# A diffusion trunk on one core: block differences and weight sums on VectorE, row sums in four column groups

## The chip, the core and the metric

The kernel runs on one core of a Trainium2 chip. A core has TensorE (PE in the profile), which multiplies matrices; VectorE (DVE) and ScalarE (ACT) for elementwise work; GpSimd (POOL), also elementwise here; and SyncE (SP), which issues most of the transfers. Each engine takes the instructions of its own queue in order; semaphores make one engine wait for another. TensorE reads its operands from the on-chip memory SBUF and writes to accumulators in PSUM, which VectorE or ScalarE have to read out before their place is used again. The metric is the device time of one execution in microseconds; less is better.

## The reference

One layer (DEPTH = 1) of a generator of latents: 2048 latent tokens and 256 context tokens of width 1024. An HGRN2 mixer with two scan directions over eight heads is followed by a gated FFN with a convolution; each part is preceded by an RMS norm with a shift and a scale that come from a conditioning vector.

```python
m_l = (sc_lat @ w_ada[l] + b_ada[l])[:, None, :]
sh1, sc1, g1, sh2, sc2, g2 = jnp.split(m_l, 6, axis=-1)
hl = modulate(rmsnorm(lat, norm_g[l, 0]), sh1, sc1)
...
# in the mixer:
q, zf_fwd, zf_bwd, v, g = jnp.split(h @ w_in, 5, axis=-1)
...
lat = lat + g1 * yl
hl = modulate(rmsnorm(lat, norm_g[l, 1]), sh2, sc2)
lat = lat + g2 * conv_ffn(hl, ffn_w_up[l], ffn_conv_w[l], ffn_conv_b[l], ffn_w_down[l])
```

The change touches two things: the projections to `v` and `g` (columns 3 and 4 of the five parts of `w_in`), which the early stage computes ahead of the mixer, and the rows `g1`, `sh2`, `sc2` and `g2` of the modulation, which are needed later.

## The kernel before

**Exact products from three passes.** Each operand is split into a high part that TensorE multiplies exactly enough and the rest: `split` (L80, L81) lets ScalarE copy the source to the high part and VectorE subtract that from the source. A product is then three matmuls: high by high, high by low, low by high.

**The early stage** (`early`, about the first 420 us) first computes the shift and scale of the first norm (L352, four column groups of 32 partitions into one accumulator), then normalizes, transposes and modulates the tokens, and multiplies them by the `v` and `g` weights of the heads. The multiplication is a Strassen-Winograd scheme of two by two blocks: tokens in two units by weights of a pair of heads, the inner width of 1024 in two halves. Seven block products per pair of heads take the place of eight; for them one needs differences of token blocks and sums of weight blocks:

- `differences(j)` (L450 to L455): for each of four slices j, two differences on VectorE (L450, L451), whose results are split at once into the factors T2 and T1, and two more on POOL (L454, L455), written over the tokens in `hm0`, which are split later into T3 and T4.
- `Blocks.sums` (L217, L218) makes S1 and S2 of the weight blocks, `sum3` (L223) makes S3 in the place of one raw block and `sum4` (L228) S4 in the place of S2. All four work on 128 x 512 floats, and all run on POOL.
- `product(g, p, n)` runs one block product of twelve matmuls (L515, L517, L518) for the pair p and then reads the accumulator out, with ScalarE (L526, L530, L544) or with an addition on VectorE (L546, L549, L551, L557). The accumulators have four tags (za, zc, zd, tr) with two buffers each. `turned_out` transposes a finished block on TensorE (L476) some steps later, copies it with ScalarE (L477) and stores it.

**Two halves.** The list `todo` holds the products. The first half (g = 1) takes tokens 1024 to 2047 with seven pairs of heads: four of `v` (`vs`) and three of `g` (`gs`). The second (g = 0) takes tokens 0 to 1023 with eight pairs, after `turn_over`. Raw weights come in by DMA into a few reused tiles (`load_raws`, L577); `prepare` asks for sums and splits four products ahead (`LOOK`). During the first half `side_tokens` also normalizes and transposes tokens 0 to 1023 (L130, L132, L139, L143), takes their differences on VectorE (L682 to L687) and stores them to memory, from where `load_factor` brings them back for the second half. The scale of a norm is a power on POOL (L76) between two VectorE instructions (L75, L132).

**The order** of each engine's queue isn't the order of the program text alone: a scheduler orders instructions by need and by its own estimate of when their inputs are there; `issue_after`, `behind_of` and `then` add edges that place one behind another, and `at(clock, f)` places work at a count of products.

**The later modulation rows** (`ada_rest`) run beside the second half: for each of four rows, VectorE accumulates eight slices of `w_ada` times the conditioning vector into `acc` (L725, L727); the row is the sum of `acc` over its 128 partitions. TensorE makes it by multiplying with a column of ones, in two products of 512 columns (L735), each into an accumulator of tag tr; ScalarE copies each to SBUF (L736), and SP stores the row to memory (L737).

Of the kernel before, what the change touches and what calls it, by code (L numbers as in the profile page):

```python
# [11 lines left out]
F32 = mybir.dt.float32  # L12
# [3 lines left out]
AF = mybir.ActivationFunctionType  # L16
OP = mybir.AluOpType
# [28 lines left out]
def body(ctx, tc, a, out):  # L46
    nc = tc.nc
    pe, act, dve, pool, sp = nc.tensor, nc.scalar, nc.vector, nc.gpsimd, nc.sync
# [4 lines left out]
    m_rows = [dr.tile([1, D], F32, name=f"m_row{i}") for i in range(4)]  # L53
# [13 lines left out]
    def small(name, shape=(128, 8), dt=F32):  # L67
        return cst.tile(list(shape), dt, name=name)
# [10 lines left out]
    def split(h, l, src):  # L79
        i = act.activation(h, src, AF.Copy)  # L80
        j = dve.tensor_tensor(l, src, h.bitcast(F32), OP.subtract)  # L81
        return i.ins, j.ins
# [13 lines left out]
    def pool_(stack, name, bufs=1, **kw):  # L96
        return stack.enter_context(tc.tile_pool(name=name, bufs=bufs, reuse_waits="tile", **kw))
# [66 lines left out]
    G_PLAIN = NH - 2  # L164
# [39 lines left out]
    class Blocks:  # L204


        def __init__(self, ring):
            self.ring, self.w = ring, {}

        def raws(self, raw):  # L210
            self.raw = raw
# [19 lines left out]
        def split(self, n, w=None):  # L231
            if n in self.w:
                return
            if n == "S3" and n not in self.src:
                self.sum3()
            if n == "S4" and n not in self.src:
                self.sum4("S2")
            if w is None:
                w = self.ring()
            self.w[n] = w  # L240
            return split(w[:, 0], w[:, 1], self.src[n])
# [3 lines left out]
            return act.activation(hm, tp, AF.Identity, bias=B1[m][:, k:k + 1], scale=A1[m][:, k:k + 1])  # L245
        return dve.tensor_scalar(hm, tp, A1[m][:, k:k + 1], B1[m][:, k:k + 1], OP.mult, OP.add)

    ones = small("ones", (128, 1))
    pool.memset(ones, 1.0)

    def early():
# [4 lines left out]
        pb = pool_(ce, "pb", 2)  # L256
# [15 lines left out]
        def factor_tile(n):  # L272
            f = left_place if n in LEFT_PLACE else place
            return f({**PLACE, **LEFT_PLACE}[n], TOK, F32R, "r" + n)

        def half_tile(tag, bufs, name=None):
            return pb.tile([128, UT, 128], F32, name=name or tag, tag=tag, bufs=bufs)
# [71 lines left out]
        for k in range(KT):  # L349
            for c in range(4):  # L350
                n = 2 * k + c // 2
                pe.matmul(mp[32 * c:32 * c + 32], silp[:, k],  # L352
                          ada[n // 4][:, n % 4, c % 2 * 512:(c % 2 + 1) * 512],
                          start=k == 0, stop=k == KT - 1, skip_group_check=True)
# [24 lines left out]
        def split_ctx(g):  # L379
            b = cxt[:, g // 2, :, :, 2 * (g % 2):2 * (g % 2) + 2]  # L380
            return split(b[:, :, 0], b[:, :, 1], hmc[g].rearrange("p k s n -> p s k n"))
# [8 lines left out]
        ps = pool_(ce, "pse", 2, space=PSUM)  # L390
# [22 lines left out]
        def z_tile(tag):  # L413
            return ps.tile([128, UT, 128], F32, name=tag, tag=tag)

        hm0 = px.tile([128, KT, UT, 128], F32, name="hm0", tag="X", bufs=1)
        rhs = {}

        def unit0(k):

            tp = z_tile("tr")
            turn_tok(tp.rearrange("p (i j) n -> p i j n", i=1), range(HT, HT + UT), (k,))
            hm = hm0[:, k]
            i = modulated(hm, tp, k, 0, k % 2 == 0).ins
            b = block(0, k // 4)[:, :, :, k % 4]
            return split(b[:, :, 0], b[:, :, 1], hm)
# [17 lines left out]
        def differences(j):  # L444

            if j == 0:
                for n in ("T2", "T1", "T3", "T4"):
                    rhs[n] = factor_tile(n)
            a12, a22 = hm1[j], hm1[j + 4]
            dve.tensor_tensor(a12, a12, hm0[:, j], OP.subtract)  # L450
            dve.tensor_tensor(a22, a22, a12, OP.subtract)  # L451
            put_split("T2", j, a22)
            put_split("T1", j, a12)
            pool.tensor_tensor(hm0[:, j], a22, hm0[:, j], OP.subtract)  # L454
            pool.tensor_tensor(hm0[:, j + 4], hm0[:, j + 4], a22, OP.subtract)  # L455

        def put_split(n, j, src):
            split(rhs[n][:, :, 0, j], rhs[n][:, :, 1, j], src)
# [32 lines left out]
        for p in range(4):  # L491
# [10 lines left out]
            z = z_tile("zc").rearrange("p (i s) n -> p i s n", i=2)  # L502
            for i in range(2):
                context_row(p, i, z[:, i])
            o = half_tile("out", 4)
# [72 lines left out]

        class Heads(Blocks):

            def __init__(self, ty, h):
                super().__init__(ring)
                self.ty, self.h, self.z, self.summed = ty, h, {}, False

            def first_half(self, tile):
# [4 lines left out]
            def prepare(self, n):  # L590
                if LEFT[n] in self.w:
                    return
                if n[0] == "T" and not self.summed:
                    self.summed = True
                    self.sums(pool, *[pb.tile([128, 4, 128], F32, name=n, tag=n) for n in ("s1", "s2")])
                self.split(LEFT[n])

        todo = []
        vs = [Heads(3, 2 * i) for i in range(4)]
        for p, b in zip(vs, vb):  # L600
            p.w.update({n: b.w[n] for n in ("A11", "A12")})
        gs = [Heads(4, h) for h in range(0, G_PLAIN, 2)]
        for p in gs[0:2]:
            p.first_half(rawp.tile([128, D], F32, name="raw", tag="raw"))
        at(c0 + 21, lambda: gs[2].first_half(lp.tile([128, D], F32, name="raw", tag="stg", bufs=1)))
# [13 lines left out]
        todo += [(1, p, n) for n in FACTORS[2:] for p in gs[0:2]]  # L619
        turn_over = len(todo)  # L620
        for i, (ty, h) in enumerate(((3, 0), (3, 4), (4, 0), (4, 4))):
            both = [Heads(ty, h), Heads(ty, h + 2)]
            loads[len(todo) - 12] = both, i % 2 == 0
            todo += [(0, p, n) for n in FACTORS for p in both]

# [4 lines left out]
        def unit1_step(i):  # L630
            k = (0, 4, 1, 5, 2, 6, 3, 7)[i]
            then(unit1, k)
            if i % 2:
                differences(k - 4)
# [16 lines left out]
        def side_tokens(j, now):  # L651
# [41 lines left out]
            for i, (u, g) in enumerate(((0, 0), (0, 1), (1, 0), (1, 1))):  # L693
                at(now + 8 + 2 * i, lambda u=u, g=g: turn(u, g))
            at(now + 17, differences)
            at(now + 19, differences2)

# [5 lines left out]
        def spare_raw():  # L703
            if not spare:
                spare.extend([hq.tile([128, 4, D], F32, name="spare", tag="cxt", bufs=1), 0])
            spare[1] += 1
            return spare[0][:, (spare[1] - 1) % 4]

        def ada_rest():

            def load(n):
                i, k = divmod(n, KT)
                raw = spare_raw()
                sp.dma_start(raw, a["w_ada"][k * 128:(k + 1) * 128, (2 + i) * D:(3 + i) * D])
                return raw

            ahead = [load(n) for n in range(2)]
            yield
            for i in range(4):
                acc_ = lp.tile([128, D], F32, name="acc", tag="stg", bufs=1)  # L720
                for k in range(KT):
                    raw = ahead.pop(0)
                    s_ = sil[:, k:k + 1]
                    if k:
                        dve.scalar_tensor_tensor(acc_, raw, s_, acc_, OP.mult, OP.add)  # L725
                    else:
                        dve.tensor_scalar(acc_, raw, s_, None, OP.mult)  # L727
                    if k == KT - 1:
                        row = spare_raw()[0:1]
                    if KT * i + k + 2 < 4 * KT:  # L730
                        ahead.append(load(KT * i + k + 2))
                    yield
                for n in range(2):
                    z = ps.tile([1, 512], F32, name="z", tag="tr")
                    pe.matmul(z, ones, acc_[:, n * 512:(n + 1) * 512], start=True, stop=True)  # L735
                    act.activation(row[:, n * 512:(n + 1) * 512], z, AF.Copy)  # L736
                sp.dma_start(m_rows[i], row)  # L737
                yield

        rest = ada_rest()  # L740
        factor_raw = []

# [134 lines left out]
    first_out = []  # L877

    early()
    clock, at, run, tick = ticking()  # L880
    Sf = hp.tile([128, NH, 128], F32, name="Sf", tag="Sf", bufs=1)
# [559 lines left out]
    def cols(u, odd):  # L1441

        return u[:, 1:1 + HALF].rearrange("p (j o n) -> p j o n", o=2, n=128)[:, :, odd]
# [307 lines left out]
    ps = pool_(fp, "psa", 2, space=PSUM)  # L1751
# [94 lines left out]
    ring = {}  # L1846
# [53 lines left out]
    for g, (half, s, n, q, pairs) in enumerate(todo):  # L1900
# [9 lines left out]
        if n == "B11":  # L1910
            z = bank["a", q] = ps.tile([128, HJ, 128], F32, name="za", tag="za")
# [3 lines left out]
        elif n == "T2":  # L1915
            z = ps.tile([128, HJ, 128], F32, name="zb", tag="zb")
            acc_mm(z, w, r, True)
            dve.tensor_tensor(u2s[q], u2s[q], z, OP.add)
        elif n == "T1":
            z = bank["d", q] = ps.tile([128, HJ, 128], F32, name="zd", tag="zd")  # L1920
            acc_mm(z, w, r, True)
            uvs[q] = u_tile(wk, "v")
            i = dve.tensor_tensor(cols(uvs[q], 1), u2s[q], z, OP.add).ins
# [4 lines left out]
        elif n == "T3":  # L1928
            z = bank["c", q] = ps.tile([128, HJ, 128], F32, name="zc", tag="zc")
            acc_mm(z, w, r, True)  # L1930
            dve.tensor_tensor(cols(uvs[q], 1), cols(uvs[q], 1), z, OP.add)
        elif n == "B21":
            z = bank["a", q]
# [3 lines left out]
        elif n == "B22":  # L1937
            z = bank["d", q]
            acc_mm(z, w, r, False)
            dve.tensor_tensor(cols(ugs[q], 1), u2s[q], z, OP.add)  # L1940
        else:
            z = bank["c", q]
# [15 lines left out]
    ps = pool_(fb, "psb", 8, space=PSUM)  # L1958
# [176 lines left out]
    for s in range(N):  # L2135
        ph, c = divmod(s, NC)
# [62 lines left out]
    for i, (j, cs) in enumerate(pieces):  # L2199
        prepare_last(i + 2)  # L2200
        if cs.start == 0:
            z = ps.tile([128, 512], F32, name="y", tag="y")
# [36 lines left out]
```

## Time and profile before

| | |
|---|---|
| median of three runs | 2717.66 us |
| lowest and highest | 2716.46 and 2718.87 us |
| the profiled execution | 2719.17 us |
| its span from the first to the last instruction | 2717.5 us |
| TensorE busy in the span | 98% |
| granted TensorE clock, mean | 0.994 |
| TensorE busy, 0 to 34 us (first shift and scale) | 18.07 of 34 us |

In a row of instruction groups one reads line, engine, operation, result and inputs, shapes, the count, then busy time and the mean duration in nanoseconds, and last the idle time of that engine just before them with what ended it. A row of the waits names the waiting engine and instruction, then what it waited for, the total in us, the number and the longest. A timeline row has start, duration, engine and line; the idle time before it and what ended it stand in brackets. "w<-raw" means that tile w is written from tile raw. An instruction that takes longer than others of its shape was slowed down while it ran; that isn't shown as a wait.

### The profile page before, as it was taken

Reading aid. Unit: us, or ns where it says so; the run is one execution under the profiler, and the core shown is the slowest. Engines: PE = TensorE matmul, PEld = TensorE weight load, DVE = VectorE, ACT = ScalarE, POOL = GpSimd, SP = SyncE. Lnnn points to the kernel's source line nnn. Section 1 sums busy time; section 2 is a strip of 40 time slices with the busy share of each in tenths; the row PEclk is TensorE's granted clock in tenths of the full one; section 3 lists DMA queues with packets and bytes.
Section 4 is the critical chain, followed back from the end, with each engine's and each line's share of the span. In section 5 each row is a group of like instructions: output and inputs, shape, how many; then the busy total and the mean of one; then the engine's idle time right before and its main releaser. Section 6 shows DMA issues by size and latency. Waiting matters only on the chain.

```text
span 2717.5 us, 41952 instructions
## 1 busy us (share of the span) xinstructions
PE 2665.1 (98%) x15880; PEld 2224.9 (82%) x15880; DVE 2077.1 (76%) x2941; ACT 1162.8 (43%) x1987; POOL 679.9 (25%) x956
## 2 busy tenths in 40 slices
PE   7898999999999999999999999999999999999998
PEld 4677778888888888888888888888888888888887
DVE  4867767778777777778987888777877777578896
ACT  4655343333332222335666444443444444333444
POOL 1523241222222222211121543343434440000001
PEclk9899999999999999999999999999999999999999
DMA  8668646434456353538888222127222234988553
GB/s 328 246 236 277 237 145 232 135 126 148 138 193 211 120 191 128 161 106 299 292 315 318 93 93 93 63 86 301 94 82 74 78 94 142 313 277 289 197 187 132
DMA packets 249826, 493.92 MB, mean 182 GB/s; under 512 B 27284, under 2 KB 140308, under 8 KB 239000
## 3 DMA queue, kind: packets, MB, share of 16 engines
q1 hardware_dynamic: 244904, 482.00, 51.8%
q10 hardware_dynamic: 4720, 9.24, 0.9%
q8 instruction: 125, 2.05, 0.3%
q14 instruction: 77, 0.63, 0.1%
HBM read 331.51 MB, written 159.66 MB: 181 GB/s over the span
## 4 chain that ended last, share of the span: by engine, by line
PE 87%; DVE 1%; DMA 1%; issue 0%; ACT 0%; POOL 0%; ACTq 0%; SPq 0%; POOLq 0%; DVEq 0%
PE z L935 7%; PE z L934 7%; PE z L933 7%; PE y L2052 5%; PE y L2053 5%; PE y L2051 5%; PE zc L1450 3%; PE zc L1453 3%; PE zc L1452 3%; PE za L1453 3%; PE zd L1453 3%; PE zd L1450 3%; PE za L1452 3%; PE zd L1452 3%; PE za L1450 3%; PE kv L1130 2%
## 5 line engine op out<-in xcount | busy, mean ns | idle before, releaser
L81 DVE TENSOR_TENSOR w<-raw,w 128x512 fp32r<-128x512 f32 (+1 forms) x262 | 218.3, 836 | 74.0 <-ACT w L80 71.8
L80 ACT ACTIVATE w<-raw 128x512 fp32r<-128x512 f32 (+1 forms) x262 | 174.6, 672 | 180.9 <-PE zd L1453 75.0
L2052 PE MATMUL y<-w,mh 128*128 128x512 f32 x600 | 233.5, 389 | 0.2 <-DVE w L81 0.2
L2053 PE MATMUL y<-w,ml 128*128 128x512 f32 x600 | 233.4, 389 | 0.0
L2051 PE MATMUL y<-w,mh 128*128 128x512 f32 x600 | 233.2, 389 | 0.0
L81 DVE TENSOR_TENSOR w<-s,w 128x512 fp32r<-128x512 f32 x171 | 159.8, 939 | 62.6 <-ACT w L80 61.2
L933 PE MATMUL z<-tok,w 128*128 128x512 f32 x512 | 207.4, 405 | 0.0
L935 PE MATMUL z<-tok,w 128*128 128x512 f32 x512 | 200.2, 391 | 0.0
L934 PE MATMUL z<-tok,w 128*128 128x512 f32 x512 | 199.8, 390 | 0.0
L80 ACT ACTIVATE w<-s 128x512 fp32r<-128x512 f32 x171 | 106.5, 630 | 186.0 <-POOL s L218 82.8
L977 DVE TENSOR_TENSOR_SCAN S<-F,d 128x528 f32<-128x528 f32 (+1 forms) x80 | 91.7, 1146 | 118.1 <-ACT F L959 118.1
L1450 PE MATMUL zc<-rT,w 128*128 128x512 f32 x352 | 137.0, 389 | 1.8 <-DMA rT<-rhs1T 1.8
L1453 PE MATMUL zc<-rT,w 128*128 128x512 f32 x352 | 136.9, 389 | 0.0
L1452 PE MATMUL zc<-rT,w 128*128 128x512 f32 x352 | 136.9, 389 | 0.0
L217 POOL TENSOR_TENSOR s<-raw 128x512 f32<-128x512 f32 x57 | 94.8, 1662 | 167.8 <-DMA raw<-in_w_up_dram 132.4
L2052 PEld LDWEIGHTS y<-w,mh 128*128 128x128 f32 x600 | 112.6, 188 | 24.1 <-DVE w L81 0.6
L2051 PEld LDWEIGHTS y<-w,mh 128*128 128x128 f32 x600 | 112.6, 188 | 23.9 <-ACT w L80 0.3
L2053 PEld LDWEIGHTS y<-w,ml 128*128 128x128 f32 x600 | 112.6, 188 | 23.0
L1136 ACT ACTIVATE sk<-kv 128x256 f32<-128x256 f32 x64 | 24.6, 384 | 248.4 <-DVE states L1133 152.0
L1452 PE MATMUL za<-rB,w 128*128 128x512 f32 x336 | 130.7, 389 | 0.0
L1453 PE MATMUL za<-rB,w 128*128 128x512 f32 x336 | 130.7, 389 | 0.0
L1450 PE MATMUL za<-rB,w 128*128 128x512 f32 x336 | 130.7, 389 | 0.0
(466 smaller groups left out, 7700.5 us busy)
## 6 DMA issues: line engine op xcount, KB each, us to landing
w<-w SPq DMA_DIRECT2D x48, 1024.0 KB, 5.4
raw<-in_w_up_dram SPq DMA_DIRECT2D x88, 512.0 KB, 3.8
raw<-in_w_in_dram SPq DMA_DIRECT2D x67, 512.0 KB, 5.2
lr<-m SPq DMA_DIRECT2D x49, 512.0 KB, 4.9
m<-r SPq DMA_DIRECT2D x66, 256.0 KB, 3.9
spare<-in_w_ada_dram SPq DMA_DIRECT2D x32, 512.0 KB, 4.7
kq<-stash SPq DMA_DIRECT2D x15, 1024.0 KB, 6.7
og<-stash SPq DMA_DIRECT2D x30, 512.0 KB, 4.7
```

Of the source, the lines that this page charges most:

```text
L80: i = act.activation(h, src, AF.Copy)
L81: j = dve.tensor_tensor(l, src, h.bitcast(F32), OP.subtract)
L217: eng.tensor_tensor(s1, a21, a22, OP.add)
L933: pe.matmul(z, w[:, 0, k], h, start=k == 0, stop=False, skip_group_check=True)
L934: pe.matmul(z, w[:, 0, k], l, start=False, stop=False, skip_group_check=True)
L935: pe.matmul(z, w[:, 1, k], h, start=False, stop=k == KT - 1, skip_group_check=True)
L1450: pe.matmul(o, w[:, 0, k], r[:, :, 0, k], start=start and k == 0, stop=False, skip_group_check=True)
L1452: pe.matmul(o, w[:, 0, k], r[:, :, 1, k], start=False, stop=False, skip_group_check=True)
L1453: i = pe.matmul(o, w[:, 1, k], r[:, :, 0, k], start=False, stop=k == 3, skip_group_check=True)
L2051: pe.matmul(z, lh, rh, start=start, stop=False, skip_group_check=True)
L2052: pe.matmul(z, lh, rl, start=False, stop=False, skip_group_check=True)
L2053: pe.matmul(z, ll, rh, start=False, stop=stop, skip_group_check=True)
```

## The change

1. The two later differences of each slice (L454, L455) are issued on VectorE instead of POOL.
2. `Blocks` gets an engine for its sums. The seven pairs of the first half are made with VectorE (sums, S3 and S4); the eight pairs of the second half stay on POOL, as do the four `Blocks` of the context.
3. The sum of a later row over partitions is four products of 256 columns, each into its own group of 32 partitions of one accumulator, with eight columns of ones as weights; ScalarE copies eight partitions of each group in four instructions, and one DMA stores four pieces of 256 floats from partitions 0, 32, 64 and 96.

```diff
-        def __init__(self, ring):
-            self.ring, self.w = ring, {}
+        def __init__(self, ring, eng=pool):
+            self.ring, self.w, self.eng = ring, {}, eng
...
-                self.sum3()
+                self.sum3(self.eng)
...
-                self.sum4("S2")
+                self.sum4("S2", self.eng)
...
-    ones = small("ones", (128, 1))
+    ones = small("ones", (128, 8))
...
-            pool.tensor_tensor(hm0[:, j], a22, hm0[:, j], OP.subtract)
-            pool.tensor_tensor(hm0[:, j + 4], hm0[:, j + 4], a22, OP.subtract)
+            dve.tensor_tensor(hm0[:, j], a22, hm0[:, j], OP.subtract)
+            dve.tensor_tensor(hm0[:, j + 4], hm0[:, j + 4], a22, OP.subtract)
...
-            def __init__(self, ty, h):
-                super().__init__(ring)
+            def __init__(self, ty, h, eng):
+                super().__init__(ring, eng)
...
-                    self.sums(pool, *[pb.tile([128, 4, 128], F32, name=n, tag=n) for n in ("s1", "s2")])
+                    self.sums(self.eng, *[pb.tile([128, 4, 128], F32, name=n, tag=n) for n in ("s1", "s2")])
...
-        vs = [Heads(3, 2 * i) for i in range(4)]
+        vs = [Heads(3, 2 * i, dve) for i in range(4)]
...
-        gs = [Heads(4, h) for h in range(0, G_PLAIN, 2)]
+        gs = [Heads(4, h, dve) for h in range(0, G_PLAIN, 2)]
...
-            both = [Heads(ty, h), Heads(ty, h + 2)]
+            both = [Heads(ty, h, pool), Heads(ty, h + 2, pool)]
...
-                        row = spare_raw()[0:1]
+                        row = spare_raw()[:, 0:256]
...
-                for n in range(2):
-                    z = ps.tile([1, 512], F32, name="z", tag="tr")
-                    pe.matmul(z, ones, acc_[:, n * 512:(n + 1) * 512], start=True, stop=True)
-                    act.activation(row[:, n * 512:(n + 1) * 512], z, AF.Copy)
-                sp.dma_start(m_rows[i], row)
+                z = ps.tile([128, 256], F32, name="z", tag="tr")
+                for n in range(4):
+                    pe.matmul(z[32 * n:32 * n + 8], ones, acc_[:, n * 256:(n + 1) * 256],
+                              start=True, stop=True, skip_group_check=True)
+                for n in range(4):
+                    act.activation(row[32 * n:32 * n + 8], z[32 * n:32 * n + 8], AF.Copy)
+                sp.dma_start(m_rows[i].rearrange("o (n c) -> (o n) c", n=4), row[0:128:32])
```

## The prediction

> **What bounds the kernel now.** I read the page's busy table first, then the windows view by stage, then TensorE's waits in the stage that the change touches, and last the timelines of the engines behind each wait.
>
> ```profile
> PE 2665.1 (98%) x15880; PEld 2224.9 (82%) x15880; DVE 2077.1 (76%) x2941; ACT 1162.8 (43%) x1987; POOL 679.9 (25%) x956
> ```
>
> ```profile
> 60.00:260.00 200.00, 179.08 (x862) 145.81 (x861) 143.94 (x190) 122.24 (x242) 73.68 (x52) 0.95 0.70 245
> 260.00:390.00 130.00, 130.00 (x585) 101.39 (x584) 97.08 (x112) 49.05 (x86) 43.26 (x26) 1.00 0.64 212
> 390.00:2717.00 2327.00, 2316.07 (x14201) 1953.30 (x14199) 1812.61 (x2588) 964.40 (x1611) 554.81 (x860) 1.00 0.50 170
> 110.00:126.00 16.00, 10.90 (x42) 8.24 (x41) 14.01 (x14) 13.12 (x30) 11.15 (x7) 0.71 0.84 292
> ```
>
> The columns of a window are its length, then busy time of PE, PEld, DVE, ACT and POOL, the granted TensorE clock, the DMA share and GB/s. TensorE is the bound: 2665.1 of the span's 2717.5 us. From 260 us on it has no idle time to speak of, so there only less TensorE work helps, and an idle microsecond removed ahead of it passes through to the end. From 60 to 260 us, where both groups of moved sums run, it idles 200 − 179.1 = 20.9 us; the worst stretch is 110 to 126, with 5.1 us idle and a granted clock of 0.71. Those 20.9 us are nearly all in nine waits:
>
> ```profile
> PE tr L476 <- DVE out L557: 4.9, 1, 4.9
> PE tp L139 <- ACT side L143: 3.6, 2, 3.3
> PE za L515 <- ACT u L544: 3.0, 1, 3.0
> PE za L515 <- DVE u L546: 2.4, 1, 2.4
> PE tr L476 <- DVE hm L246: 2.0, 1, 2.0
> PE zd L515 <- DVE out L549: 2.0, 1, 2.0
> PE za L515 <- ACT w L80: 1.5, 1, 1.5
> PE tr L299 <- DVE hm L246: 1.0, 1, 1.0
> PE tr L299 <- ACT out L477: 0.7, 1, 0.7
> ```
>
> No wait names POOL, but VectorE stands behind five of them, and the timelines show POOL behind VectorE.
>
> **Part 1: 36 operations move from POOL to VectorE.** These are eight differences (L454, L455) and four sums (L217, L218, L223, L228) for each of the seven pairs of the first half.
>
> ```profile
> L228 POOL TENSOR_TENSOR s<-raw,s 128x512 f32<-128x512 f32 x7 | 11.4, 1626 | 10.8 <-DVE w L81 9.3 <-DVE rs L75 1.5
> L217 POOL TENSOR_TENSOR s<-raw 128x512 f32<-128x512 f32 x7 | 11.0, 1566 | 26.7 <-DMA raw<-in_w_in_dram 26.7
> L223 POOL TENSOR_TENSOR raw<-raw 128x512 f32<-128x512 f32 x7 | 10.8, 1538 | 0.3
> L218 POOL TENSOR_TENSOR s<-s,raw 128x512 f32<-128x512 f32 x7 | 9.9, 1416 | 4.7 <-DVE w L81 4.5
> L454 POOL TENSOR_TENSOR hm<-hm,hm 128x512 f32<-128x512 f32 x4 | 7.1, 1769 | 45.2 <-DVE hm L451 45.2
> L455 POOL TENSOR_TENSOR hm<-hm,hm 128x512 f32<-128x512 f32 x4 | 6.5, 1618 | 0.0
> ```
>
> ```profile
> L81 DVE TENSOR_TENSOR rT<-hm,rT 128x512 fp32r<-128x512 f32 x16 | 17.5, 1115 | 4.8 <-ACT rT L80 4.8
> L451 DVE TENSOR_TENSOR hm<-hm 128x512 f32<-128x512 f32 x4 | 2.7, 683 | 0.0
> L687 DVE TENSOR_TENSOR side<-side 128x512 f32<-128x512 f32 x2 | 3.5, 1764 | 0.0
> ```
>
> On POOL one such operation takes 1.4 to 1.8 us, on VectorE 0.683 (L451, same shape, clean). POOL loses about 56.7 us, VectorE gains 36 x 0.683 = 24.6. But VectorE gets something back: where a POOL operation runs beside a VectorE one with both inputs in SBUF, the latter takes about 1.77 instead of 0.68 (L687), so each meeting costs it 1.1 us; the sixteen rT splits alone lose 16 x (1.115 − 0.683) = 6.9. If two thirds of the 36 meet such an instruction, VectorE's total comes out even. So the gain isn't less VectorE work; it is that work moving out of five crowded places and a shorter chain to what needs the result. Wait by wait:
>
> ```profile
> 83.48 1.58 DVE L132 TENSOR_SCALAR side<-side,rs 128x1024 f32<-128x1024 f32 x2 [1.46 <-POOL rs L76]
> 103.53 1.79 DVE L81 TENSOR_TENSOR stg<-hm,stg 128x512 fp32r<-128x512 f32 x1
> 105.24 1.76 DVE L81 TENSOR_TENSOR rT<-hm,rT 128x512 fp32r<-128x512 f32 x1
> 129.08 1.78 DVE L683 TENSOR_TENSOR side<-side 128x512 f32<-128x512 f32 x1
> 134.19 1.75 DVE L687 TENSOR_TENSOR side<-side 128x512 f32<-128x512 f32 x1
> 173.33 0.75 DVE L132 TENSOR_SCALAR x<-x,rs 128x1024 f32<-128x1024 f32 x1 [2.79 <-POOL rs L76]
> 221.32 3.46 DVE L81 TENSOR_TENSOR w<-raw,w 128x512 fp32r<-128x512 f32 x2
> 226.37 0.68 DVE L557 TENSOR_TENSOR out<-u,zc 128x512 f32<-128x512 f32 x1
> ```
>
> - *1.0, hm L246:* the norm's scale (L76, on POOL) stood behind two differences, and VectorE waited 1.46. Without them that goes and two operations come (1.4), but one blocked split ahead gets 0.7 shorter: I take **0.9** (0 to 1.0).
> - *2.0, hm L246:* two blocked instructions (103.53, 105.24) give back 2.2, two differences cost 1.4, and three sums might also be put ahead (2.0). **1.0** (0 to 2.0).
> - *2.4, u L546:* from 129.08 to the end of 134.19 four blocked instructions in a row give back 4.4; four sums of the next pairs cost 2.7 if they all stay ahead. Earlier blocked ones help too: the whole **2.4** (0 to 2.4).
> - *2.0, out L549:* VectorE waited 2.79 for a scale queued on POOL behind four sums. Some 2 us of that go; four sums (2.7) come, in part into idle time before. **1.5** (0 to 2.0).
> - *4.9, out L557:* the two splits at 221.32 took 3.46 instead of 1.3. But what blocked them is mostly the *second* half's sums, which stay on POOL:
>
> ```profile
> 214.60 1.33 POOL L217 TENSOR_TENSOR s<-raw 128x512 f32<-128x512 f32 x1 [8.47 <-DMA raw<-in_w_in_dram]
> 220.81 1.75 POOL L217 TENSOR_TENSOR s<-raw 128x512 f32<-128x512 f32 x1
> 167.15 1.43 POOL L217 TENSOR_TENSOR s<-raw 128x512 f32<-128x512 f32 x1 [14.66 <-DMA raw<-in_w_in_dram]
> ```
>
>   The last pair's sums start at 214.60, when the weights land, and their chain of two gets some 1.3 us shorter; two of the later blockers also go. **2.0** (0 to 4.9).
> - *3.6, side L143:* ScalarE is late here, since its splits wait for the differences:
>
> ```profile
> 106.48 0.63 ACT L80 ACTIVATE rT<-hm 128x512 fp32r<-128x512 f32 x1 [1.03 <-POOL hm L455]
> 116.72 0.63 ACT L80 ACTIVATE rT<-hm 128x512 fp32r<-128x512 f32 x1 [1.04 <-POOL hm L455]
> ```
>
>   Both waits of about 1 us go; after that ScalarE's own queue is the limit (13.1 busy of 16). **1.5** (0 to 3.6).
> - *3.0, 1.5, 0.7* end with ScalarE work in which neither POOL nor a sum stands: **0**.
>
> That is 0.9 + 1.0 + 2.4 + 1.5 + 2.0 + 1.5 = 9.3 us. Less idle time also means less time at a low clock: **0.6** (0 to 3, the 4.6 us-equivalents that 0.71 over 16 us lacks being mostly idle time). Against it stands a new kind of wait: a sum queued on VectorE holds everything behind it until its weights land. On POOL the sums waited 26.7 us for weights, and nothing there was urgent. On VectorE the evictions L546 to L557 stand behind them, TensorE's accumulators behind those, and ScalarE's later work. I expect most sums to be placed near the products that need them, as weights landed by then, and one short hold: **−1.0** (0 to −12, see below). Part 1 gives 8.9.
>
> [...]
>
> **Part 2: the four row sums (L735).**
>
> ```profile
> 294.25 1.88 PE L735 MATMUL z<-acc,ones 128*1 128x512 f32 x4
> 296.05 0.50 PE L515 MATMUL zc<-rT,w 128*128 128x512 f32 x1
> 16.70 1.06 PE L352 MATMUL mps<-wada,silp 128*32 128x512 f32 x8 [0.68 <-DMA wada<-in_w_ada_dram]
> ```
>
> Now two products make four passes, one after the other: 296.05 − 294.25 = 1.80 us per row. L352 already uses four column groups: eight passes of 512 columns in 1.06. With 256 columns, eight passes take about 0.53, with some switching 0.60. All of it lies on the bound engine in a stage without idle time: 4 x 1.2 = **4.8 us** (−1, if the groups went one after the other with their weight loads, to 5.2). ScalarE copies four pieces instead of two; nearest row:
>
> ```profile
> L1136 ACT ACTIVATE sk<-kv 128x256 f32<-128x256 f32 x64 | 24.6, 384 | 248.4 <-DVE states L1133 152.0
> ```
>
> Four of 0.38 for two of about 0.59 is 0.4 more per row; ScalarE is busy 49 of 130 us there, which hides it; without that cover it would cost 1.5 in all. The row's store sits on SP's queue as before, in four pieces; its readers come tens of microseconds later: 0. One accumulator in place of two eases their turn: 0.
>
> [...]
>
> **The sum.** 8.9 + 4.8 = 13.7 us. The profiled execution took 2719.17 (span 2717.5), 1.5 above the median of 2717.66; off the median it gives **2704.0**, −0.5%.
>
> **The rivals.**
> - *The waits stay.* VectorE's total comes out even, so a sum put ahead of each urgent eviction eats what the blocking gave back; only part 2 lands: 2717.7 − 4.8 = 2712.9. For it: VectorE is busy 14.0 of 16 us in the worst stretch. Against: four of the six waits show more given back than added. Chance 0.17.
> - *All go.* The six waits vanish whole (15.9 of the 20.9), with 2 us of clock: 2717.7 − 15.9 − 2 − 4.8 = 2695.0. Chance 0.13.
> - *The column groups don't overlap.* 2717.7 − 8.9 = 2708.8. Against: L352. Chance 0.07.
> - *VectorE waits for weights (slower).* The sums at 167.15 and 214.60 waited 14.66 and 8.47 for their DMA. If they stand as early in VectorE's queue, evictions wait too. TensorE has two accumulators of each kind, two products of twelve matmuls at 130/585 us, so it loses what exceeds about 5.4: 9.3 + 3.1 = 12.4; with the other waits unchanged, 2717.7 + 12.4 − 4.8 = 2725.3. It decides from a hold of some 5.4 us with an eviction behind it. For it: one queue, in order. Against: VectorE has much urgent work at that time that an order by need puts first. Chance 0.11.
>
> **How the numbers follow.** The forecast has 0.52, with 2699 to 2711 as its own range. The range that leaves out the slower case and the far ends of the others is 2694 to 2717. About 0.2% (5.4 us) is what a measurement of this kernel can tell from no change, so faster means under 2712.2. Faster: nearly all of the forecast (0.50), all of "all go" (0.13), most of "no overlap" (0.06), a third of "the waits stay" (0.05): 0.74. Slower: most of the last rival, 0.09. The rest, 0.17, is the same.
>
> **What would show it.** Right: TensorE's idle time between 60 and 260 us falls from 20.9 to about 12, the 2.4 wait for L546 is gone, VectorE instructions of 1.7 us appear only beside the second half's sums, and L735's group of a row takes about 0.6. Wrong: a VectorE wait for "DMA raw" of several microseconds with a TensorE wait behind it; L735 passes that start 0.2 apart; a ScalarE wait in the place of a VectorE one with the idle time unchanged.

## The result, and the profile after

Three comparisons put the changed kernel 12 to 18 us under the kernel before. In one execution of the first of them the matmuls of the costliest groups took 1.09 to 1.14 us on average, where those of the kernel before took 0.39 to 0.41 (9945.56 us in all): it counts among the five of that median, but not in the ratio, and the trace shown is that of a later execution of the same kernel.

| kernel | median us | before, same comparison | ratio | 95% interval |
|---|---|---|---|---|
| changed, first | 2706.74 | 2718.87 | 0.9953 | 0.9939 to 0.9968 |
| changed, second (`again`) | 2702.61 | 2720.34 | 0.9937 | 0.9924 to 0.9951 |
| changed, third (`changed_side`) | 2702.76 | 2718.72 | 0.9942 | 0.9929 to 0.9956 |

The intervals overlap; by the middle ratio the gain is 15.8 us of 2718. The forecast was 13.7.

The windows view of the changed kernel (`again`; columns as before) and TensorE's waits in the stage:

```profile
60.00:260.00 200.00, 189.00 (x930) 155.19 (x930) 153.73 (x236) 126.94 (x253) 24.14 (x21) 0.96 0.74 262
260.00:390.00 130.00, 129.97 (x619) 104.85 (x618) 97.59 (x121) 52.34 (x98) 45.84 (x37) 1.00 0.62 199
```

```profile
PE za L515 <- ACT u L544: 4.6, 1, 4.6
PE tp L139 <- ACT side L143: 2.6, 2, 1.9
PE za L515 <- ACT w L80: 2.2, 1, 2.2
PE za L518 <- DVE w L81: 0.9, 1, 0.9
PE tr L476 <- DVE out L557: 0.7, 1, 0.7
```

Idle time from 60 to 260 us fell from 20.9 to 11.0 us, and no wait for L546, L549 or hm L246 is left. But the wait for L544, put down as untouched, has grown from 3.0 to 4.6, that for w L80 from 1.5 to 2.2, and one for a split on VectorE is new. VectorE's instructions in the stage (rows of the groups by form, 60 to 220 us):

```profile
L81 DVE TENSOR_TENSOR rT<-hm,rT 128x512 fp32r<-128x512 f32 x16 | 10.7, 686 | 2.9 <-ACT rT L80 2.8
L81 DVE TENSOR_TENSOR rB<-fraw,rB 128x512 fp32r<-128x512 f32 x8 | 7.7, 1016 | 3.5 <-ACT rB L80 3.5
L217 DVE TENSOR_TENSOR s<-raw 128x512 f32<-128x512 f32 x7 | 4.7, 685 | 1.4 <-DMA raw<-in_w_in_dram 1.4
L455 DVE TENSOR_TENSOR hm<-hm,hm 128x512 f32<-128x512 f32 x4 | 2.7, 686 | 0.0
L687 DVE TENSOR_TENSOR side<-side 128x512 f32<-128x512 f32 x2 | 1.4, 688 | 0.0
```

The sixteen rT splits take 686 ns instead of 1115, L687 688 instead of 1764: with the moved operations off POOL these are no longer slowed. The eight rB splits still are: they take 1016 on average, and the slow ones run from 212 us on, beside the second half's sums, which stay on POOL. The moved operations cost 685 each, as estimated. On the whole VectorE neither gained nor lost:

```profile
PE 2659.0 (98%) x15896; PEld 2223.5 (82%) x15896; DVE 2075.6 (77%) x2977; ACT 1163.0 (43%) x1995; POOL 626.6 (23%) x920
```

2075.6 us busy against 2077.1, with 36 instructions more. The row sum, in the timeline of TensorE:

```profile
282.48 0.62 PE L735 MATMUL z<-acc,ones 128*8 128x256 f32 x8
283.03 0.50 PE L515 MATMUL zc<-rT,w 128*128 128x512 f32 x1
```

It holds TensorE for 283.03 − 282.48 = 0.55 us, where it held it for 1.80.

### The profile page after: what moved, and what is told of

Same layout as the page of the kernel before. It is cut to its first block, busy times and chain, and to the rows that moved or that the text cites. A ratio compares the mean times of both kernels' runs of the same rounds, so it can differ in the third digit from the quotient of the medians.

```text
span 9943.8 us, 41974 instructions
## 1 busy us (share of the span) xinstructions
PE 9928.6 (100%) x15896; PEld 5804.9 (58%) x15896; DVE 2066.7 (21%) x2977; ACT 1184.7 (12%) x1995; POOL 553.3 (6%) x920
## 3 DMA queue, kind: packets, MB, share of 16 engines
q8 instruction: 125, 2.05, 0.1%
## 4 chain that ended last, share of the span: by engine, by line
PE 100%; issue 0%; DMA 0%; ACT 0%; DVE 0%; SPq 0%; POOL 0%; POOLq 0%
PE z L935 7%; PE z L936 7%; PE z L937 7%; PE y L2053 5%; PE y L2054 5%; PE y L2055 5%; PE zd L1452 3%; PE zc L1452 3%; PE zd L1454 3%; PE zc L1454 3%; PE zc L1455 3%; PE zd L1455 3%; PE za L1454 3%; PE za L1452 3%; PE za L1455 3%; PE y L1556 2%
## 5 line engine op out<-in xcount | busy, mean ns | idle before, releaser
L2054 PE MATMUL y<-w,mh 128*128 128x512 f32 x600 | 659.3, 1099 | 0.0
L2053 PE MATMUL y<-w,mh 128*128 128x512 f32 x600 | 658.9, 1099 | 0.0
L2055 PE MATMUL y<-w,ml 128*128 128x512 f32 x600 | 651.1, 1085 | 0.0
L935 PE MATMUL z<-tok,w 128*128 128x512 f32 x512 | 584.4, 1141 | 0.0
L936 PE MATMUL z<-tok,w 128*128 128x512 f32 x512 | 560.3, 1094 | 0.0
L937 PE MATMUL z<-tok,w 128*128 128x512 f32 x512 | 560.3, 1094 | 0.0
L2054 PEld LDWEIGHTS y<-w,mh 128*128 128x128 f32 x600 | 263.6, 439 | 232.8 <-issue 232.8
L2053 PEld LDWEIGHTS y<-w,mh 128*128 128x128 f32 x600 | 254.3, 424 | 242.2 <-issue 241.8
L2055 PEld LDWEIGHTS y<-w,ml 128*128 128x128 f32 x600 | 253.3, 422 | 231.6 <-issue 231.0
L1454 PE MATMUL zc<-rT,w 128*128 128x512 f32 x352 | 386.8, 1099 | 0.0
L1452 PE MATMUL zc<-rT,w 128*128 128x512 f32 x352 | 386.6, 1098 | 0.0
L1455 PE MATMUL zc<-rT,w 128*128 128x512 f32 x352 | 382.3, 1086 | 0.0
L1454 PE MATMUL za<-rB,w 128*128 128x512 f32 x336 | 369.2, 1099 | 0.0
L1452 PE MATMUL za<-rB,w 128*128 128x512 f32 x336 | 369.2, 1099 | 0.0
L1455 PE MATMUL za<-rB,w 128*128 128x512 f32 x336 | 364.6, 1085 | 0.0
L81 DVE TENSOR_TENSOR w<-raw,w 128x512 fp32r<-128x512 f32 (+1 forms) x262 | 195.8, 751 | 713.3 <-ACT w L80 711.1
L80 ACT ACTIVATE w<-raw 128x512 fp32r<-128x512 f32 (+1 forms) x262 | 174.8, 671 | 1378.0 <-PE zd L1455 495.0
L937 PEld LDWEIGHTS z<-tok,w 128*128 128x128 f32 x512 | 218.6, 427 | 193.6 <-issue 193.6
L935 PE MATMUL z<-rB,w 128*128 128x512 f32 x288 | 327.2, 1136 | 0.0
L935 PEld LDWEIGHTS z<-tok,w 128*128 128x128 f32 x512 | 226.9, 443 | 170.7 <-issue 167.9
L936 PEld LDWEIGHTS z<-tok,w 128*128 128x128 f32 x512 | 228.4, 446 | 164.1 <-issue 163.8
L936 PE MATMUL z<-rB,w 128*128 128x512 f32 x288 | 315.3, 1095 | 0.0
```

Of the source, the lines that this page charges most:

```text
L935: pe.matmul(z, w[:, 0, k], h, start=k == 0, stop=False, skip_group_check=True)
L936: pe.matmul(z, w[:, 0, k], l, start=False, stop=False, skip_group_check=True)
L937: pe.matmul(z, w[:, 1, k], h, start=False, stop=k == KT - 1, skip_group_check=True)
L1452: pe.matmul(o, w[:, 0, k], r[:, :, 0, k], start=start and k == 0, stop=False, skip_group_check=True)
L1454: pe.matmul(o, w[:, 0, k], r[:, :, 1, k], start=False, stop=False, skip_group_check=True)
L1455: i = pe.matmul(o, w[:, 1, k], r[:, :, 0, k], start=False, stop=k == 3, skip_group_check=True)
```

## The experiments

**Each part alone.** `rows_only` is the kernel before with the diff of point 3 only, `dve_only` with points 1 and 2 only.

> The changed kernel once more, for a profile of an undisturbed execution. By the forecast (part 1 gives 8.9 us, part 2 4.8) some 13 us under the kernel before, TensorE idle from 60 to 260 us down from 20.9 to about 12, a row sum L735 about 0.6 us instead of 1.8. If the waits stay, idle time near 20 and the whole gain from L735 and below 6 us.

> Part 2 alone (row sums in four column groups), sums and differences on POOL as before. If the groups overlap: 4.8 us under the kernel before, about 2713. If they go one after the other: within 1 us of before. The idle time from 60 to 260 us stays at 20.9 by both.

> Part 1 alone (differences and sums of the first half on VectorE), row sums as before. By the forecast 8.9 us under the kernel before, about 2709, with idle time near 12 from 60 to 260 us. If the waits stay: within 2 us of before. If the moved sums make VectorE wait for weights: slower than before by up to 12, with a VectorE wait for the raw weights.

In one comparison (before 2720.34): `rows_only` 2715.11, ratio 0.9982 (0.9973 to 0.9991); `dve_only` 2709.39, ratio 0.9960 (0.9947 to 0.9972); both parts 2702.61. That is 5.2 and 11.0 us alone and 17.7 together, so the parts add up within the intervals. TensorE's idle time from 60 to 260 us stays at 20.9 in `rows_only` and falls to 10.5 in `dve_only`. "The waits stay" has fallen: it gave part 1 nothing, and part 1 alone gives 11.0 (7.6 to 14.4).

**What makes the row sum short.** `one_group` keeps the passes of 256 columns and the eight columns of ones, but puts all four products in the first column group:

```diff
-                z = ps.tile([128, 256], F32, name="z", tag="tr")
-                for n in range(4):
-                    pe.matmul(z[32 * n:32 * n + 8], ones, acc_[:, n * 256:(n + 1) * 256],
-                              start=True, stop=True, skip_group_check=True)
+                for n in range(2):
+                    z = ps.tile([8, 512], F32, name="z", tag="tr")
+                    for m in range(2):
+                        pe.matmul(z[:, m * 256:(m + 1) * 256], ones,
+                                  acc_[:, n * 512 + m * 256:n * 512 + (m + 1) * 256],
+                                  start=True, stop=True, skip_group_check=True)
...
```

> The changed kernel, but with the four products of 256 columns all in the first column group (two accumulators of 8 x 512, two copies, one row stored). If the gain of part 2 is the overlap of groups, it is gone: a row sum takes eight passes one after the other, 1.7 us or more, and the time is 4 to 5 us above the changed kernel. If the gain comes from the shorter passes or the wider weights, the time stays within 1 us of the changed kernel.

2708.03 us (ratio 0.9960, 0.9948 to 0.9973), 5.4 above the changed kernel in the same comparison; the two intervals just overlap. Its row sum, in the timeline of TensorE:

```profile
281.28 1.89 PE L736 MATMUL z<-acc,ones 128*8 128x256 f32 x8
283.10 0.50 PE L515 MATMUL zc<-rT,w 128*128 128x512 f32 x1
```

1.82 us with the same eight passes: the overlap of the groups is the whole gain of part 2, 4 x (1.82 − 0.55) = 5.1 us.

**Which moved operations.** `diff_only` is the kernel before with L454 and L455 on VectorE, `sums_only` with point 2 alone.

> The kernel before with only the eight differences (L454, L455) on VectorE. If they stand behind the first waits, the two for hm L246 (1.0 and 2.0) go and those around 110 to 126 us get shorter by 1 to 3: 3 to 6 us under before. If the sums alone matter: within 2 us of before.

> The kernel before with only the sums of the first half on VectorE. If the waits for L546 (2.4), L549 (2.0) and L557 (4.9) come from POOL's sums, they go, with some 1.5 us of half clock after each, and the wait for L544 grows: 4 to 9 us under before. If the differences alone matter: within 2 us of before.

Before 2720.63; `diff_only` 2714.47, ratio 0.9979 (0.9971 to 0.9988); `sums_only` 2711.92, ratio 0.9966 (0.9955 to 0.9976). Both count. Their 6.2 and 8.7 us make 14.9, more than the 11.0 of `dve_only` in the other comparison; whether they overlap or the comparisons differ isn't settled. The rows of TensorE's waits (60 to 400 us) that bear on this, first of `diff_only`, then of `sums_only`:

```profile
PE tp L139 <- ACT side L143: 6.0, 2, 5.7
PE tr L476 <- DVE out L557: 4.5, 1, 4.5
PE zd L515 <- DVE out L549: 1.9, 1, 1.9
```

```profile
PE tp L139 <- ACT side L143: 5.2, 2, 4.9
PE za L515 <- ACT u L544: 4.6, 1, 4.6
PE tr L476 <- DVE hm L246: 1.9, 1, 1.9
PE tr L299 <- DVE hm L246: 1.8, 1, 1.8
```

The waits divide as the reasons said: L549 and L557 belong to the sums, hm L246 to the differences, and L546 is in neither list, so either move is enough for that one. The rows also show what a list of waits hides: with the differences moved, TensorE begins to wait for the side tokens 6.7 us earlier (109.26 instead of 115.96), the copies L143 begin only 4.3 earlier, and the wait is 6.0 instead of 3.6. With the sums moved it is 5.2: there the copies begin no earlier than before. So here the waits removed came back in part at the next place where something else is late.

**Where the gain was given back.** The wait for L544 grew. Rows of the changed kernel, from the timelines of ScalarE, VectorE and POOL:

```profile
238.73 0.63 ACT L80 ACTIVATE rB<-fraw 128x512 fp32r<-128x512 f32 x1 [2.29 <-DMA fraw<-part]
240.31 1.65 ACT L80 ACTIVATE rB<-fraw 128x512 fp32r<-128x512 f32 x3
243.87 0.63 ACT L526 ACTIVATE out<-out 128x512 f32<-128x512 f32 x1 [1.39 <-issue]
244.40 0.58 ACT L544 ACTIVATE u<-za 128x512 f32<-128x512 f32 x1
```

```profile
240.95 2.23 DVE L81 TENSOR_TENSOR rB<-fraw,rB 128x512 fp32r<-128x512 f32 x2 [0.27 <-ACT rB L80]
243.11 0.68 DVE L557 TENSOR_TENSOR out<-u,zc 128x512 f32<-128x512 f32 x1
```

```profile
240.77 1.27 POOL L228 TENSOR_TENSOR s<-raw,s 128x512 f32<-128x512 f32 x1 [16.11 <-DVE w L81]
```

ScalarE's queue has the split of a factor (rB) ahead of the read-out L544, and that split waits for its transfer. Behind it VectorE's two splits take 2.23 instead of some 1.3 while a sum of the *second* half (L228) runs on POOL; L557 follows, L526 starts when L557 has ended, and L544 stands behind L526. Before the change L544 also stood behind a split that waited for its transfer, another one (rT at 257.43, 2.05 us). Two edits test the two links, POOL's sums and ScalarE's order. `all_dve` moves the second half's sums too:

```diff
-            both = [Heads(ty, h, pool), Heads(ty, h + 2, pool)]
+            both = [Heads(ty, h, dve), Heads(ty, h + 2, dve)]
```

`behind_u` leaves them on POOL, asks for the splits of the factors B22 and T4 nine products later and puts them behind the read-outs on ScalarE:

```diff
-                act.activation(s["u2"], z, AF.Copy)
+                i = act.activation(s["u2"], z, AF.Copy)
+                if g == 0:
+                    u_read.append(i.ins)
...
+        def fraw_split(n, j, f, raw):
+            if n in ("B22", "T4") and u_read:
+                with tc.issue_after(u_read[min(1, len(u_read) - 1)]):
+                    split(f[:, j, 0], f[:, j, 1], raw[:, j])
+            else:
+                split(f[:, j, 0], f[:, j, 1], raw[:, j])
...
-                at(clock[0] + 9 + j, lambda j=j: split(f[:, j, 0], f[:, j, 1], raw[:, j]))
+                at(clock[0] + (18 if n in ("B22", "T4") else 9) + j, lambda j=j: fraw_split(n, j, f, raw))
```

> The changed kernel with the second half's sums on VectorE too. If only waits of TensorE count, there are hardly any from 260 us on, and the time stays within 2 us of the changed kernel. If 32 further operations crowd VectorE (97.6 of 130 us busy in that stage), new waits for L546 to L557 appear and it is 3 us or more above the changed kernel.

> The changed kernel, but the splits of the last two factors loaded for the second half (B22, T4) are queued on ScalarE behind the two read-outs L544 that TensorE waits for (4.6 us in the changed kernel, 3.0 before). If that wait comes from ScalarE's order (a split that waits for its DMA stands ahead of the read-out), it goes with the half clock after it: 4 to 7 us under the changed kernel. If the loads themselves are the limit, TensorE waits later, at the products that need these factors (B22, T4), and the time is within 2 us of the changed kernel.

`all_dve` 2697.44, `behind_u` 2697.92 (before 2720.63, ratio 0.9919, 0.9905 to 0.9932, for both): some 5 us under the changed kernel's other comparisons. For `all_dve` that was neither of the expected outcomes: the reason given for "within 2 us" was that few waits are left from 260 us on, but the second half's sums are already at work at 240. Rows of `all_dve`, ScalarE and then TensorE:

```profile
235.42 1.15 ACT L80 ACTIVATE rB<-fraw 128x512 fp32r<-128x512 f32 x2 [1.05 <-DMA fraw<-part]
237.52 1.14 ACT L80 ACTIVATE rB<-fraw 128x512 fp32r<-128x512 f32 x2
239.10 0.63 ACT L526 ACTIVATE out<-out 128x512 f32<-128x512 f32 x1 [0.45 <-ACT rB L80]
239.64 0.58 ACT L544 ACTIVATE u<-za 128x512 f32<-128x512 f32 x1
243.64 0.58 ACT L544 ACTIVATE u<-za 128x512 f32<-128x512 f32 x1
```

```profile
244.27 0.50 PE L515 MATMUL za<-rB,w 128*128 128x512 f32 x1 [0.98 <-ACT u L544]
```

L544 runs at 239.64 instead of 244.40, and TensorE doesn't wait for it; the wait of 1.0 us that is left is for the next read-out, at 243.64. Most of this isn't the two slowed splits at 240.95, which lose about 1 us: the transfer itself comes earlier, and the first split rB starts at 235.42 instead of 238.73. The second half's sums had slowed four other splits before, and SP issues the next load of a factor behind those. VectorE and SP, changed kernel first (POOL has L217 and L223 from 212.99 to 216.43 there), then `all_dve`:

```profile
212.42 5.16 DVE L81 TENSOR_TENSOR rB<-fraw,rB 128x512 fp32r<-128x512 f32 x4
217.60 0.53 SPq L751 DMA_DIRECT2D fraw<-part  x1
```

```profile
211.79 2.49 DVE L81 TENSOR_TENSOR rB<-fraw,rB 128x512 fp32r<-128x512 f32 x4
214.31 0.53 SPq L751 DMA_DIRECT2D fraw<-part  x1
```

That load is issued 3.3 us earlier, and the split rB starts 3.3 us earlier; the loads in between weren't followed one by one. In `behind_u`, where the sums stay on POOL, TensorE waits 0.3 us for the same read-out (L546 there):

```profile
PE za L515 <- ACT u L546: 0.3, 1, 0.3
```

If the two edits cut the same chain, they don't add:

> The changed kernel with both of the last two edits: the second half's sums on VectorE too, and the splits of B22 and T4 behind the read-outs L544. Both removed the same wait for L544 (4.6 us and its half clock), so the gains don't add: if that is so, 5 to 8 us under the changed kernel, the 1.0 left of that wait gone. If they are separate, 9 to 11 under it.

`combined` 2698.37 against 2716.35, ratio 0.9926 (0.9913 to 0.9940), no further than each alone (by the ratios 3 to 4 us under the changed kernel, a little less than the 5 to 8 expected); the wait for L544 is gone there. So it was one chain with two links, sums that make a factor's split late and a queue in which that split holds up the read-out, and cutting either is enough. The changed kernel and `all_dve` side by side:

> The changed kernel a third time, beside the next one on the same chip. Two comparisons so far put it 12.8 and 17.7 us under the kernel before; if both are draws of one effect, this one lies between, near 15. Only a value near one of the two would speak for a difference between chips.

> The kernel with all sums on VectorE, beside the changed kernel on the same chip. If it takes away the wait for L544 and its half clock (7.0 us in the two traces), it is 5 to 7 us under the changed kernel here too. If the difference before was one between chips, within 2 us.

2702.76 and 2696.62 (before 2718.72; `all_dve` 0.9925, 0.9913 to 0.9938): 6.1 us between the medians; the two intervals still overlap a little. `all_dve` computes the same as the changed kernel; in its two comparisons it was 23 and 22 us under the kernel before.

**What is left at 111 to 121 us.** The changed kernel still idles 5.7 us there (side L143, w L80, w L81). I read it as ScalarE's queue with its sixteen copies L143. `side12` is `combined` with the first block of side tokens turned twelve steps later:

```diff
-            at(c0 + (44, 73, 88, 98)[j], lambda j=j: side_tokens(j, c0 + 52 + (0, 29, 49, 69)[j]))
+            at(c0 + (44, 73, 88, 98)[j], lambda j=j: side_tokens(j, c0 + 52 + (12, 29, 49, 69)[j]))
```

With this edit the second block's load overwrites the first block's tokens before they are turned, so that the parts stored for the first block hold other tokens; the work is the same.

> The combined kernel with the first block of side tokens turned twelve steps later (its sixteen copies L143 on ScalarE come after the splits w<-raw and w<-s instead of ahead of them). If ScalarE's queue is what is left of the waits at 110 to 121 us (side L143, w L80, w L81: 5.8 us and the half clock), most of it goes: 4 to 8 us under the combined kernel. If the weights' splits are late for another reason, or the copies then hold up other read-outs, the waits move on by some microseconds and the time is within 2 us of the combined kernel.

2695.12 against `combined`'s 2698.37 in the same comparison (ratios to before 0.9920, 0.9907 to 0.9932, and 0.9926): 3.3 us, inside the overlap of the two intervals, and neither of the expected outcomes. It isn't less waiting: TensorE's idle time from 60 to 260 us is 8.1 instead of 6.3. Its larger wait, and the row of ScalarE behind it:

```profile
PE za L515 <- ACT w L80: 7.5, 1, 7.5
```

```profile
117.00 0.63 ACT L80 ACTIVATE w<-raw 128x512 fp32r<-128x512 f32 x1 [4.57 <-DMA raw<-in_w_in_dram]
```

The copies are out of the way, and now the first split w<-raw waits 4.57 us for raw weights. The copies only covered that wait. The profile puts the 4.57 down to the load of the third `g` pair (L586; L590 in this kernel, issued at 108.33), which goes into the tile that the last `stg` slice leaves free. In the changed kernel the same load, issued at 109.53, took 8.0 us to land, about as long as the copies lasted (to 117.84). That an earlier load would help isn't shown: one into a place of its own wasn't tried.

## Why the prediction was right, and where its terms were off

- **What bounds the kernel:** right. TensorE stays at 98%, and what it gains ahead of 260 us reaches the end. From the first product of the stage to one late in the second half:

```profile
61.91 0.47 PE L515 MATMUL za<-tok,w 128*128 128x512 f32 x1
419.89 0.39 PE L515 MATMUL zc<-rT,w 128*128 128x512 f32 x1
```

```profile
63.40 0.47 PE L515 MATMUL za<-tok,w 128*128 128x512 f32 x1
402.99 0.39 PE L515 MATMUL zc<-rT,w 128*128 128x512 f32 x1
```

  Before 357.98, changed 339.59: 18.4 us less between the same two products, with as many matmuls between them. The span fell by 16.6, because that execution began the stage 1.5 us later, in a part that the change doesn't touch.
- **The five VectorE waits** (forecast 7.8 of their 12.3): 11.6 went. L546, L549 and both of hm L246 vanished; of L557's 4.9, costed at 2.0, 0.7 is left. The step held that the second half's sums would go on blocking VectorE there. They did go on: the 0.7 stands behind a split of 1.79 us at 210.10, and the splits at 212.42 and 240.95 were slowed as well. But little of it reached TensorE at that place; it came out at L544.
- **side L143** (forecast 1.5): 1.0 in its own row. The three waits costed at nothing, since neither POOL nor a sum stood in them, went from 5.2 to 6.8, and a wait of 0.9 for w L81 is new. This step failed: L544 hangs on VectorE through L526 and L557, and on POOL through VectorE. The prediction asked only whether POOL or a sum stands in ScalarE's own work there, not what that work waits for one and two queues further back.
- **Idle time in all:** 9.3 less 1.0 for new holds was forecast, 20.9 − 11.0 = 9.9 measured. That these lie so close is partly luck: the VectorE waits gave 3.8 more than forecast, and the ScalarE waits with the new one for w L81 gave 3.0 less. The hold was small: VectorE waited 1.4 us for raw weights (the row of L217), and TensorE for none of it. The slower rival fell with that: the sums were queued near their use.
- **The clock** (forecast 0.6): the term that was sized worst. 18.4 − 9.9 − 5.0 leaves 3.5 us. Rows of TensorE's timeline after a wait, first before, then changed:

```profile
176.20 0.76 PE L515 MATMUL zd<-tok,w 128*128 128x512 f32 x1 [1.95 <-DVE out L549]
176.76 0.63 PE L517 MATMUL zd<-tok,w 128*128 128x512 f32 x1
177.19 0.63 PE L518 MATMUL zd<-tok,w 128*128 128x512 f32 x1
```

```profile
245.03 0.79 PE L515 MATMUL za<-rB,w 128*128 128x512 f32 x1 [4.55 <-ACT u L544]
245.62 0.63 PE L517 MATMUL za<-rB,w 128*128 128x512 f32 x1
250.32 0.58 PE L515 MATMUL za<-rB,w 128*128 128x512 f32 x1
250.97 0.40 PE L518 MATMUL za<-rB,w 128*128 128x512 f32 x1
```

  After these waits matmuls start 0.43 us apart instead of 0.23. At 245.03 that lasts for twelve matmuls, 5.29 us instead of about 2.7: the wait of 4.6 cost another 2.6. Three of the removed waits had such tails too (those that end at 107.78, 176.20 and 227.19; not the 2.4 at 136.59), and they should have been costed with them. TensorE's busy time times the missing share of the granted clock, summed over windows of half a microsecond from 60 to 300 us, is 8.8 us before and 6.1 in the changed kernel: 2.7 of the 3.5; the rest isn't accounted for. The prediction took what the clock lacks from 110 to 126 us (4.6) for mostly idle time; by the same windows 3.2 of it fall on busy time.
- **Part 2** (forecast 4.8): 1.80 to 0.55 per row, 5.0 in all. The forecast's 0.60 held 0.07 for switching, the author's estimate: no run shows that term by itself. What the rows show is 0.55 for the eight passes; the group starts 0.32 us after the matmul ahead of it (0.33 before the change), and the first matmul behind it takes 0.33 until the next starts (0.34 before), where others here start 0.23 apart. Four copies on ScalarE hid as said: TensorE was busy 129.97 of 130 us from 260 to 390.
- **The rivals:** "the waits stay" fell with `dve_only`, "no overlap" with L735's row, "waits for weights" with the 1.4. "All go" came nearer than its chance of 0.13 says: five of the six waits did shrink to nearly nothing, and what kept the time above its 2695 was above all the wait that grew: without it, `all_dve` took 2697.

## What to carry to other kernels

An engine off the bound can still be the cause of a wait two queues further on; where an instruction takes 1.7 us and its like 0.7, look at what the neighbour ran at that moment, and move the work out of the crowded place rather than count totals. Cost a TensorE wait with the slow matmuls that can stand behind it (2.6 us behind the 4.6 here), and expect an earlier arrival to meet the next late transfer: follow each remaining wait back through all queues before putting it down as untouched.

## What the runs showed of the hardware that wasn't expected

After a wait of 1.95 us TensorE's granted clock was 0.51; after one of 2.95 us it was 1.00. The windows view right after the two waits shown above, first before, then changed (granted clock in the third column from the end):

```profile
176.20:179.00 2.80, 2.80 (x9) 2.31 (x10) 2.80 (x4) 0.86 (x2) 1.66 (x1) 0.51 0.00 0
```

```profile
245.00:250.30 5.30, 5.27 (x12) 4.12 (x13) 4.77 (x4) 3.58 (x7) 4.53 (x3) 0.50 0.84 243
```

It was 1.00 in the 4 us ahead of either wait; afterwards it is 0.51 and 0.50. Two other waits of the kernel before, of 2.42 us (L546) and 2.95 us (L544), were followed by a clock of 1.00:

```profile
136.59:139.40 2.81, 2.81 (x12) 2.31 (x13) 1.15 (x2) 0.00 (x0) 1.30 (x1) 1.00 0.99 360
259.63:262.40 2.77, 2.77 (x12) 2.31 (x13) 2.39 (x4) 1.99 (x4) 1.50 (x1) 1.00 0.75 296
```

So the length of the wait alone doesn't decide; what else does stays open.
